# The low halves of a trunk kernel's weight pieces: a negated rounding by ScalarE and an adding transfer instead of subtractions by VectorE and GpSimd

## The chip, the core and the metric

The kernel runs on one core of a Trainium2 chip. The metric is the time of one execution on the device in microseconds (us). The kernel before takes 1647.43 us, the median of 3 runs (1647.31 to 1648.04).

## What is computed

A two-layer encoder trunk is applied to two sequences of 256 tokens with 1024 features each. All weights are fp32 and come from HBM in every run. Per layer, in the reference's words:

```
h = rmsnorm(x, attn_norm[l]);  proj = h @ w_in[l]
a_cols, b_cols, c_cols, d_cols, g_cols = jnp.split(proj, [p1, p2, p3, p4], axis=-1)
o_a, o_b, o_c, o_d = diff_mixer(a_cols ...), natten_mixer(b_cols ...), mla_mixer(c_cols ...), gqa_mixer(d_cols ...)
merged = sum over i of sigmoid(g_cols)[i] * (o_i @ w_branch[l, i])
x = x + merged @ w_out[l]
x = x + conv_ffn(rmsnorm(x, ffn_norm[l]), w_ffn_in[l], ffn_conv_w[l], ffn_conv_b[l], w_ffn_out[l])
```

## The kernel before

All 512 tokens are columns of tiles of 128 partitions x 512. Every weight matrix is cut on the host into **pieces** of 128 partitions x up to 1280 columns, laid one behind the other in one HBM tensor (`wflat`), in the order in which TensorE uses them. There are 131 pieces per layer, 262 in all; most have 1024 columns (512 KB), the gate pieces with a branch block have 1280 (640 KB).

To multiply in fp32 quality with the faster fp32r matmul, every operand is split into a rounded high half and the low rest: `wh` is the weight rounded to fp32r, `wl` is weight minus `wh`. A product is three matmuls, `wh*xh`, `wh*xl`, `wl*xh` (`mm3`, lines 296 to 299; `v_unit`, lines 455 to 457, has the weights as moving operand). So the first use of a piece's `wl` is the third matmul (in `v_unit` the second) on that piece.

One piece is one **unit** of a long list. Per layer in this order: `bq0 bk0 bq1 bk1 vb0 vb1 aq0 ak0 aq1 ak1 vd0 vd1 ve0 ve1 vf0 vf1 va0 va1` (the projections of the four attention branches), `g0` to `g31` with `cq ck cv` between (gates, with the branch products packed in), `gx0 gx1`, `wo0` to `wo7`, `fu0 fg0` to `fu21 fg21` (first half of the feed-forward), `fo0_0` to `fo7_2` (second half). A full unit of 1024 columns is 24 matmuls. The `v` pieces come in twos: unit `ve0` issues no matmul at all, and unit `ve1` issues 96 matmuls that use both pieces in turns, so that `ve1`'s data is first needed 12 matmuls after the start and `ve0`'s buffers are held almost to the end. `wo0` and `wo1` also share their matmuls.

The loop over units at lines 1206 to 1234 sets the program order: unit `i`'s matmuls, then the side work of attention, then `split_piece(i + 2)` and `load_piece(i + 5)`. `load_piece` issues the transfer of a piece from HBM into a `raw` buffer on SyncE's queue. `split_piece` (lines 279 to 294) makes `wh` by an ACTIVATE on ScalarE (line 289) and `wl` by subtraction, first half on VectorE (line 292), second half on GpSimd (line 293). `raw`, `wh` and `wl` have 3 buffers each. So piece `j` writes its `wl` into the buffer that piece `j - 3` leaves, and it can't begin before the last matmul on that piece has run. The tile framework orders the instructions of each engine by a schedule of its own; TensorE's order stays close to the program's. Each engine runs its instructions in that order.

Of the kernel before, what the change touches and what calls it, by code (L numbers as in the profile page):

```python
# [13 lines left out]
AF = mybir.ActivationFunctionType  # L14
ALU = mybir.AluOpType
# [136 lines left out]
def _piece_cols(nm):  # L152
    if nm[0] == "v":
        return {"e": 1152, "f": 1280}.get(nm[1], 1024)
    if nm == "cq":
        return 768
    if nm in ("ck", "cv"):
        return 256
    if nm[:2] == "gx":
        return 256 * (GX[int(nm[2:])][1] - GX[int(nm[2:])][0])  # L160
    if nm[0] == "g":
        return 1280 if int(nm[1:]) in GBR else 1024
    if nm[:2] == "fo":
        return 1024 if nm.endswith("_0") else 896
    return 1024
# [37 lines left out]
def trunk_kernel(ctx: ExitStack, tc: tile.TileContext, xt, wflat, gains, lams, rpb, consts, yt):  # L203
# [14 lines left out]
    V, S, G, PE = nc.vector, nc.scalar, nc.gpsimd, nc.tensor  # L218
# [11 lines left out]
    def f(ap):  # L230
        return ap.bitcast(F32)
# [30 lines left out]
    offs, o = [], 0  # L262
# [3 lines left out]
    raws, splits = {}, {}  # L266
# [12 lines left out]
    def split_piece(i, parts=1, pool_only=False):  # L279
        if i >= len(order):  # L280
            return
        n = _piece_cols(order[i][1])
        raw = raws.pop(i)
        wh = wpool.tile([128, 1280], F32R, tag="wh", name=f"wh{i}", bufs=W_BUFS)
        wl = wpool.tile([128, 1280], F32R, tag="wl", name=f"wl{i}", bufs=W_BUFS)
        w = n // parts
        for q in range(parts):
            a, b = q * w, q * w + w
            S.activation(out=wh[:, a:b], in_=raw[:, a:b], func=AF.Copy)  # L289
            c = a if pool_only else (a + b) // 2  # L290
            if c > a:
                V.tensor_tensor(out=wl[:, a:c], in0=raw[:, a:c], in1=f(wh[:, a:c]), op=ALU.subtract)  # L292
            G.tensor_tensor(out=wl[:, c:b], in0=raw[:, c:b], in1=f(wh[:, c:b]), op=ALU.subtract)  # L293
        splits[i] = (wh, wl)
# [869 lines left out]
    nc.sync.dma_start(out=lv, in_=lams.rearrange("(u n) -> u n", u=1).to_broadcast([128, DEPTH * L_ROW]))  # L1164
    prep(0, gcol(0, G_ATTN), False)
    split_piece(0, 2, True)
    load_piece(RAW_BUFS)
    for d in range(1, ND):
        prep(d, gcol(0, G_ATTN + d), False, d % 2 == 1)
        if d == 2:  # L1170
            split_piece(1, 2)
            load_piece(1 + RAW_BUFS)
# [9 lines left out]
    for i in range(2, LOOK):  # L1182
        split_piece(i)
        load_piece(i + RAW_BUFS)
# [21 lines left out]
    for i, u in enumerate(units):  # L1206
# [7 lines left out]
        wh, wl = splits.pop(i)  # L1214
# [78 lines left out]
```

## Time and profile before

| | |
|---|---|
| median of 3 runs | 1647.43 us |
| the profiled execution's own time | 1647.62 us |
| its span, first to last instruction | 1645.8 us |
| mean granted TensorE clock | 0.989 |
| TensorE (PE) busy | 1615.6 us, 98% |
| VectorE (DVE) busy | 1003.9 us, 61% |
| GpSimd (POOL) busy | 663.1 us, 40% |
| ScalarE (ACT) busy | 634.9 us, 39% |
| read from HBM | 145.77 MB |

The 1.8 us between the span and the execution's time lie around the span. PE's busy time counts pipelined matmuls whose ends are modelled: in the long stages one 512-column matmul starts every 0.227 us though each is shown with 0.39 us. What holds PE up is therefore read from its waits and from the starts of its matmuls.

### The profile page before, as it was taken

How to read it: one execution, taken by the hardware profiler on the slowest of the kernel's cores; microseconds unless marked ns; L12 is line 12 of the kernel's file. 1: busy time of each engine (PE TensorE's matmuls, PEld its weight loads, DVE VectorE, ACT ScalarE, POOL GpSimd, SP SyncE). 2: the span in 40 equal slices, each digit the busy share in tenths (PEclk: the TensorE clock that was granted, in tenths of full speed). 3: DMA queues.
4: the chain of work that ended last, by engine and by line, in shares of the span. 5: the costliest groups of instructions: out<-in, count | busy, mean ns of one | idle time of the engine just before them, and what ended most of it. 6: DMA issues, size and time to landing. Idle time of an engine off the chain costs nothing.

```text
span 1645.8 us, 21201 instructions
## 1 busy us (share of the span) xinstructions
PE 1615.6 (98%) x8035; PEld 1343.8 (82%) x8035; DVE 1003.9 (61%) x1668; ACT 634.9 (39%) x1115; POOL 663.1 (40%) x449
## 2 busy tenths in 40 slices
PE   8989999999999999999998999999999999999997
PEld 6889877878888888888886987888788888888886
DVE  7787585655776666633358675756468666656113
ACT  4555553342323333322234554544333333333321
POOL 4352223444634444444444312234465344444342
PEclk9999999999999999999998999999999999999999
DMA  6222122222323322323331121322222233232331
GB/s 218 84 68 82 55 96 80 80 78 70 107 90 103 98 95 91 98 93 106 101 109 67 55 94 57 108 84 80 77 72 98 90 103 103 90 98 88 106 95 63
DMA packets 50534, 149.24 MB, mean 91 GB/s; under 512 B 13184, under 2 KB 16128, under 8 KB 50432
## 3 DMA queue, kind: packets, MB, share of 16 engines
q1 hardware_dynamic: 49344, 146.84, 27.4%
q8 instruction: 63, 1.03, 0.3%
q10 hardware_dynamic: 1088, 1.05, 0.2%
q14 instruction: 39, 0.32, 0.1%
HBM read 145.77 MB, written 2.10 MB: 90 GB/s over the span
## 4 chain that ended last, share of the span: by engine, by line
PE 93%; DVE 3%; issue 2%; ACT 1%; POOL 0%; DMA 0%; SPq 0%; POOLq 0%; ACTq 0%; DVEq 0%
PE pf L298 10%; PE pf L299 10%; PE pf L297 10%; PE pg L297 7%; PE pg L298 7%; PE pg L299 7%; PE pfo L297 5%; PE pfo L298 5%; PE pfo L299 5%; PE pb L299 2%; PE pwo L299 2%; PE pb L298 2%; PE pwo L298 2%; PE pb L297 2%; PE pwo L297 2%
## 5 line engine op out<-in xcount | busy, mean ns | idle before, releaser
L293 POOL TENSOR_TENSOR wl<-raw,wh 128x512 fp32r<-128x512 f32 (+4 forms) x264 | 449.9, 1705 | 561.7 <-ACT wh L289 439.9
L289 ACT ACTIVATE wh<-raw 128x1024 fp32r<-128x1024 f32 (+5 forms) x264 | 281.7, 1068 | 436.4 <-PE pfo L298 132.3
L292 DVE TENSOR_TENSOR wl<-raw,wh 128x512 fp32r<-128x512 f32 (+4 forms) x262 | 254.1, 970 | 213.6 <-ACT wh L289 203.6
L297 PE MATMUL pf<-xh,wh 128*128 128x512 f32 x704 | 274.3, 390 | 0.0
L299 PE MATMUL pf<-xh,wl 128*128 128x512 f32 x704 | 273.9, 389 | 0.0
L298 PE MATMUL pf<-xl,wh 128*128 128x512 f32 x704 | 273.9, 389 | 0.0
L297 PE MATMUL pg<-xh,wh 128*128 128x512 f32 x512 | 202.2, 395 | 0.1
L298 PE MATMUL pg<-xl,wh 128*128 128x512 f32 x512 | 199.8, 390 | 0.0
L299 PE MATMUL pg<-xh,wl 128*128 128x512 f32 x512 | 199.5, 390 | 0.0
L297 PEld LDWEIGHTS pf<-xh,wh 128*128 128x128 f32 x704 | 132.2, 188 | 27.5
L298 PEld LDWEIGHTS pf<-xl,wh 128*128 128x128 f32 x704 | 132.2, 188 | 27.4
L299 PEld LDWEIGHTS pf<-xh,wl 128*128 128x128 f32 x704 | 132.2, 188 | 27.2
L297 PE MATMUL pfo<-ah,wh 128*128 128x512 f32 (+1 forms) x374 | 141.1, 377 | 0.0
L298 PE MATMUL pfo<-al,wh 128*128 128x512 f32 (+1 forms) x374 | 140.8, 376 | 0.0
L299 PE MATMUL pfo<-ah,wl 128*128 128x512 f32 (+1 forms) x374 | 140.8, 376 | 0.0
L931 POOL TENSOR_TENSOR mg<-mg,gz 128x512 f32<-128x512 f32 x48 | 64.5, 1347 | 165.4 <-DVE gz L930 165.4
L303 POOL TENSOR_TENSOR al<-fc,ah 128x512 fp32r<-128x512 f32 x44 | 57.8, 1314 | 178.9 <-ACT ah L302 178.9
L297 PEld LDWEIGHTS pg<-xh,wh 128*128 128x128 f32 x512 | 96.2, 188 | 21.1 <-issue 0.9
L299 PEld LDWEIGHTS pg<-xh,wl 128*128 128x128 f32 x512 | 96.1, 188 | 20.5
L298 PEld LDWEIGHTS pg<-xl,wh 128*128 128x128 f32 x512 | 96.3, 188 | 18.3
L952 ACT ACTIVATE gz<-gz 128x512 f32<-128x512 f32 x64 | 40.4, 631 | 127.3 <-DVE gz L951 127.2
L788 ACT ACTIVATE pr<-sc,mx 128x256 f32<-128x256 f32 x128 | 59.1, 471 | 78.6 <-DVE mx L783 78.6
(390 smaller groups left out, 2917.5 us busy)
## 6 DMA issues: line engine op xcount, KB each, us to landing
raw<-in_w_dram SPq DMA_DIRECT2D x158, 512.0 KB, 3.3
raw<-in_w_dram SPq DMA_DIRECT2D x58, 640.0 KB, 3.8
raw<-in_w_dram SPq DMA_DIRECT2D x32, 448.0 KB, 3.3
raw<-in_w_dram SPq DMA_DIRECT2D x4, 576.0 KB, 3.4
bias<-in_rpb_dram SPq DMA_DIRECT2D x32, 64.0 KB, 3.5
xall<-in_xt_dram SPq DMA_DIRECT2D x3, 512.0 KB, 7.1
raw<-in_w_dram SPq DMA_DIRECT2D x4, 256.0 KB, 4.5
out_dram<-y SPq DMA_DIRECT2D x4, 256.0 KB, 2.5
```

The lines of the kernel that those rows point to most:

```text
L289: S.activation(out=wh[:, a:b], in_=raw[:, a:b], func=AF.Copy)
L292: V.tensor_tensor(out=wl[:, a:c], in0=raw[:, a:c], in1=f(wh[:, a:c]), op=ALU.subtract)
L293: G.tensor_tensor(out=wl[:, c:b], in0=raw[:, c:b], in1=f(wh[:, c:b]), op=ALU.subtract)
L297: PE.matmul(ps, lhsT=wh, rhs=xh, start=first, stop=False)
L298: PE.matmul(ps, lhsT=wh, rhs=xl, start=False, stop=False)
L299: PE.matmul(ps, lhsT=wl, rhs=xh, start=False, stop=last)
L303: (eng or V).tensor_tensor(out=l, in0=v, in1=f(h), op=ALU.subtract)
L788: S.activation(out=p[:, qt * 256:qt * 256 + 256], in_=src[c][:, qt * 256:qt * 256 + 256], func=AF.Exp, scale=sc, bias=mx[:, i:i + 1], accu ...
L931: G.tensor_tensor(out=m, in0=m, in1=z, op=ALU.add)
L952: S.activation(out=z, in_=z, func=AF.Tanh, scale=0.5)
```

## The change

`split_piece` gets a second way, taken by every piece but the first two (which are split in two parts). ScalarE writes the rounded piece with its sign turned into `wl`, ScalarE writes the rounded piece into `wh`, and a transfer issued by GpSimd reads the piece once more from HBM and adds it onto `wl`. That makes `wl` weight minus rounded weight, as before. The two subtractions are no longer issued for these 260 pieces. Loads, buffers and matmuls are the same.

```
         w = n // parts
+        if not pool_only and parts == 1:
+            src = wflat[offs[i]:offs[i] + 128 * n].rearrange("(p n) -> p n", p=128)
+            S.activation(out=wl[:, :n], in_=raw[:, :n], func=AF.Copy, scale=-1.0)
+            S.activation(out=wh[:, :n], in_=raw[:, :n], func=AF.Copy)
+            G.dma_start(out=wl[:, :n], in_=src, accum_op=ALU.add)
+            splits[i] = (wh, wl)
+            return
         for q in range(parts):
```

Lines behind it stand 7 lower in the changed kernel. There, L289 is the negated rounding, L290 the rounding, L291 the adding transfer.

ScalarE in the first layer where TensorE goes from unit `vd1` to `ve1`, before (`wh_1121` is piece `ve1`, `wh_1149` is `vf0`; `hsq`, `vD` and `ob0h` are attention work, `ptr` a transposed tile):

```order
L814 ACTIVATE ptr<-pt 128x512
L500 ACTIVATE hsq<-psvd 128x128
L505 ACTIVATE vD<-psvd,rs 128x128
L289 ACTIVATE wh_1121<-raw_776 128x1152
L500 ACTIVATE hsq<-psvd 128x128
L505 ACTIVATE vD<-psvd,rs 128x128
L302 ACTIVATE ob0h<-po 128x256
L289 ACTIVATE wh_1149<-raw_872 128x1280
```

The same place of the changed kernel (`wl_1122` is `ve1`'s low half, `wl_1150` is `vf0`'s):

```order
L821 ACTIVATE ptr<-pt 128x512
L507 ACTIVATE hsq<-psvd 128x128
L512 ACTIVATE vD<-psvd,rs 128x128
L289 ACTIVATE wl_1122<-raw_776 128x1152
L507 ACTIVATE hsq<-psvd 128x128
L512 ACTIVATE vD<-psvd,rs 128x128
L290 ACTIVATE wh_1121<-raw_776 128x1152
L507 ACTIVATE hsq<-psvd 128x128
L309 ACTIVATE ob0h<-po 128x256
L289 ACTIVATE wl_1150<-raw_872 128x1280
```

Here the negated rounding stands where the rounding stood, and the rounding two instructions later. On GpSimd at the same place, before (`dr` and `rsh` are rotary work of attention):

```order
L594 TENSOR_TENSOR rsh<-rsh,sinr 128x512
L496 TENSOR_TENSOR dr_896<-dr_896,rtm 128x128
L293 TENSOR_TENSOR wl_1122<-raw_776,wh_1121 128x576
L496 TENSOR_TENSOR dr_897<-dr_897,rtm 128x128
L293 TENSOR_TENSOR wl_1150<-raw_872,wh_1149 128x640
```

And changed:

```order
L503 TENSOR_TENSOR dr_896<-dr_896,rtm 128x128
L291 DMA wl_1122<-in_w_dram 128x1152
L503 TENSOR_TENSOR dr_897<-dr_897,rtm 128x128
L503 TENSOR_TENSOR dr_898<-dr_898,rtm 128x128
L291 DMA wl_1150<-in_w_dram 128x1280
```

The transfer's issue takes the subtraction's place in GpSimd's order. On ScalarE in the feed-forward stage of the first layer, before (`wh_5430` is piece `fg13`, `wh_5475` is `fu14`; `fc`, `fg` and `ah` belong to the feed-forward's evacuation):

```order
L1022 ACTIVATE fg<-fc 128x512
L302 ACTIVATE ah_5392<-fc 128x512
L289 ACTIVATE wh_5430<-raw_5322 128x1024
L289 ACTIVATE wh_5475<-raw_5356 128x1024
L1016 ACTIVATE fc<-fg,gn 128x512
```

And changed:

```order
L1029 ACTIVATE fg<-fc 128x512
L290 ACTIVATE wh_5430<-raw_5322 128x1024
L309 ACTIVATE ah_5392<-fc 128x512
L289 ACTIVATE wl_5431<-raw_5322 128x1024
L290 ACTIVATE wh_5475<-raw_5356 128x1024
L289 ACTIVATE wl_5476<-raw_5356 128x1024
L1023 ACTIVATE fc<-fg,gn 128x512
```

The schedule puts the rounding ahead of the negated rounding here, against the order of the source lines; it does so for 214 of the 260 pieces, in the attention and gate stages not for all, in the stages from `wo` on for nearly all. On ScalarE where `wo0` (`wh_4037`) and `wo1` (`wh_4060`) are split, before:

```order
L952 ACTIVATE gz<-gz 128x512
L289 ACTIVATE wh_4037<-raw_3887 128x1024
L934 ACTIVATE mh_4033<-mg_2730 128x512
L952 ACTIVATE gz<-gz 128x512
L289 ACTIVATE wh_4060<-raw_3931 128x1024
```

And changed:

```order
L959 ACTIVATE gz<-gz 128x512
L290 ACTIVATE wh_4037<-raw_3887 128x1024
L289 ACTIVATE wl_4038<-raw_3887 128x1024
L941 ACTIVATE mh_4033<-mg_2730 128x512
L959 ACTIVATE gz<-gz 128x512
L290 ACTIVATE wh_4060<-raw_3931 128x1024
L289 ACTIVATE wl_4061<-raw_3931 128x1024
```

The negated rounding stands behind the rounding in both. TensorE's order differs in a handful of places of the attention stage by a few rows.

## Rows read from the trace of the kernel before

**Rows 1.** The page's first part: engine, busy us, share of span, instructions.
```profile
PE 1615.6 (98%) x8035; PEld 1343.8 (82%) x8035; DVE 1003.9 (61%) x1668; ACT 634.9 (39%) x1115; POOL 663.1 (40%) x449
```

**Rows 2.** PE's waits: us in total, times, longest us; the longest row.
```profile
PE sc L765 <- DVE sb L776: 9.3, 4, 3.1
```

**Rows 3.** Costliest groups: busy us, mean ns of one, idle before, releaser.
```profile
L293 POOL TENSOR_TENSOR wl<-raw,wh 128x512 fp32r<-128x512 f32 (+4 forms) x264 | 449.9, 1705 | 561.7 <-ACT wh L289 439.9
L289 ACT ACTIVATE wh<-raw 128x1024 fp32r<-128x1024 f32 (+5 forms) x264 | 281.7, 1068 | 436.4 <-PE pfo L298 132.3
L292 DVE TENSOR_TENSOR wl<-raw,wh 128x512 fp32r<-128x512 f32 (+4 forms) x262 | 254.1, 970 | 213.6 <-ACT wh L289 203.6
```

**Rows 4.** DMA queue (packets, MB, share of 16 engines) and issues (median us to landing).
```profile
q1 hardware_dynamic: 49344, 146.84, 27.4%
...
raw<-in_w_dram SPq DMA_DIRECT2D x158, 512.0 KB, 3.3
raw<-in_w_dram SPq DMA_DIRECT2D x58, 640.0 KB, 3.8
```

**Rows 5.** Timeline (start us, us) in the feed-forward, around piece `fg13` (first layer).
```profile
597.78 0.39 PE L299 MATMUL pf<-xh,wl 128*128 128x512 f32 x1
...
599.60 1.04 ACT L289 ACTIVATE wh<-raw 128x1024 fp32r<-128x1024 f32 x1
599.77 1.30 POOL L303 TENSOR_TENSOR al<-fc,ah 128x512 fp32r<-128x512 f32 x1 [4.25 <-ACT ah L302]
...
609.34 0.39 PE L299 MATMUL pf<-xh,wl 128*128 128x512 f32 x1
```

**Rows 6.** Timeline at `ve1`, `vf1`, `va1` (first layer): release, rounding, first use of `wl`.
```profile
98.18 0.28 PE L456 MATMUL psvd<-wl,xh 128*128 128x256 f32 x1
...
98.92 1.16 ACT L289 ACTIVATE wh<-raw 128x1152 fp32r<-128x1152 f32 x1
...
103.19 0.29 PE L456 MATMUL psve<-wl,xh 128*128 128x288 f32 x1
...
113.30 1.27 ACT L289 ACTIVATE wh<-raw 128x1280 fp32r<-128x1280 f32 x1 [1.16 <-PE psve L457]
...
119.13 0.31 PE L456 MATMUL psvf<-wl,xh 128*128 128x320 f32 x1
...
130.93 1.06 ACT L289 ACTIVATE wh<-raw 128x1024 fp32r<-128x1024 f32 x1 [1.08 <-PE psvf L457]
...
135.92 0.28 PE L456 MATMUL psva<-wl,xh 128*128 128x256 f32 x1
```

**Rows 7.** Timeline at `wo0` and `wo1` (first layer): roundings, first uses of `wl`.
```profile
411.64 1.04 ACT L289 ACTIVATE wh<-raw 128x1024 fp32r<-128x1024 f32 x1
...
416.47 1.99 ACT L289 ACTIVATE wh<-raw 128x1024 fp32r<-128x1024 f32 x2
...
417.52 0.39 PE L299 MATMUL pwo<-mh,wl 128*128 128x512 f32 x1
...
420.92 0.39 PE L299 MATMUL pwo<-mh,wl 128*128 128x512 f32 x1
```

**Rows 8.** Timeline at the last piece, `fo7_2`: rounding, first use of `wl`.
```profile
1617.02 0.95 ACT L289 ACTIVATE wh<-raw 128x896 fp32r<-128x896 f32 x1 [3.81 <-PE pfo L298]
...
1622.63 0.28 PE L299 MATMUL pfo<-ah,wl 128*128 128x256 f32 x1
```

**Rows 9.** Attention timeline of PE and DVE; then one stretch by engine, clock, DMA.
```profile
71.33 0.68 DVE L292 TENSOR_TENSOR wl<-raw,wh 128x512 fp32r<-128x512 f32 x1
...
76.86 0.38 PE L765 MATMUL sc<-bk1h,bq1h 64*128 64x256 f32 x1 [1.58 <-DVE sb L776]
...
80.05 1.89 DVE L595 TENSOR_TENSOR rc<-rc,rsh 128x512 f32<-128x512 f32 x1 [1.34 <-POOL rsh L594]
...
90.81 0.58 PE L765 MATMUL sc<-bk1h,bq1h 64*128 64x256 f32 x1 [3.05 <-DVE sb L776]
...
78.24:81.66 3.42, 3.42 (x19) 3.42 (x18) 2.08 (x3) 1.09 (x4) 2.92 (x3) 0.50 0.01 2
```

## The prediction

> **What bounds the kernel now.** I read the busy times first: TensorE is busy for 98% of the span, no other engine for more than 61% [rows 1]. The changed kernel has the same matmuls, so freeing VectorE and GpSimd buys time only where TensorE waits for them. The list of TensorE's waits says how much: its longest row is 9.3 us in four waits, for VectorE in the attention stages [rows 2]. The second thing to read is therefore not who is relieved but how early `wl` is ready, because `wl` stands in front of every third matmul. Three buffers let piece `j` begin its `wl` only when piece `j - 3` is done with, so all the work on `wl` must fit between that release and the first matmul that reads it. I read this budget from timelines of the feed-forward, of the attention projections, of `wo` and of the last piece [rows 5 to 8].
>
> **What is taken away.** 264 subtractions on GpSimd (449.9 us) and 262 on VectorE (254.1 us), but for those of the first two pieces [rows 3]. Nearly all of it is off the path. On the path it counts at two places per layer: VectorE reaches `sb` late and TensorE waits 1.58 and 3.05 us for it [rows 9]. Ahead of the first wait VectorE did two subtractions of 0.68 us [rows 9], so 1.4 us of that go. Ahead of the second stand one subtraction, about 0.7 us, and a rotary add that took 1.89 us, three times the length of an ordinary 512-column VectorE operation of 0.68 us, while GpSimd subtracted beside it [rows 9]; without both the wait loses about 2.0 us. After the first wait the granted clock fell to 0.50, that is 1.2 GHz, for 3.42 us in which TensorE was busy throughout [rows 9]; at 2.4 GHz half of that, 1.7 us, would have done. If the wait is short enough the fall goes too. Together 1.4 + 2.0 + 1.7 = 5.1 us a layer, 10 us in all. The bounds are 0 (ScalarE's longer queue puts the same time back) and 16 us (both waits, 4.6 us, vanish with 3.4 us of slow clock a layer).
>
> **What is added on ScalarE.** 260 activations of about 1.07 us [rows 3], 278 us on an engine that is 39% busy: no bound. But each lies in `wl`'s own chain, and where the rounding is placed ahead of it (214 pieces) there are two activations in the chain, not one. The rounded halves' own readiness moves by one activation at most and is needed later than the sum below; I count nothing for it.
>
> **What is added on GpSimd and the queues.** 260 issues in place of the subtractions. No DMA is issued from GpSimd in this trace, so its cost has to be bounded: 0 from below, and from above the 1.7 us of the subtraction it replaces [rows 3]. I take 1.0 us. What is queued behind an issue on GpSimd, `mg`, `al` and `dr` work, waited behind the subtraction before, so nothing is counted there. The waiting for ScalarE moves with it.
>
> **The adding transfer.** It is the new last link of the chain, and no row shows one. Nearest is the plain load of a piece: 3.3 us from issue to landing for 512 KB, 3.8 us for 640 KB [rows 4]. The queue's row gives the part that scales: 27.4% of 1645.8 us is 451 us for 146.84 MB, 3.07 us per MB, 1.6 us for 512 KB (0.524 MB) and 2.0 us for 640 KB. An add needs the old value, so bytes from two places for every byte written. From below it costs as much as a plain load. I take one load's landing plus the time of a second transfer: 3.3 + 1.6 = 4.9 us (640 KB: 5.8; 576 KB, between the two: 5.2; 448 KB: 4.7). It also meets traffic: ScalarE's last read of `raw` frees that buffer, and the load of the piece three further on (1.6 us) then starts on the same 16 engines. I take half, 0.8 us. The delay from the end of the negated rounding to landed data, call it D, is 1.0 + 4.9 + 0.8 = 6.7 us for 512 KB (640 KB 7.6; 576 KB 7.0; 448 KB 6.5). Its bounds are 3.3 us (no issue time, a plain load, no meeting) and 1.7 + 4.9 + 1.6 = 8.2 us, more if the add itself is slow.
> The Trainium skill, "Collectives: The Full Stack", section on why ReduceScatter is half of AllGather, measured an adding transfer at 1/1.93 of a copy's rate, for two reads on one ring. By that the second transfer would cost 0.93 x 1.6 = 1.5 us in place of 1.6, and the sum would hardly change; no run here shows it.
>
> **Where D fits.** Feed-forward, piece `fg13`: TensorE leaves the buffer at 597.78 + 0.39 = 598.2, and `wl` is first read at 609.34 [rows 5]. In the changed order ScalarE does the rounding, then `ah`, which was over when GpSimd took it at 599.77, then the negated rounding: 599.8 + 1.05 = 600.8. GpSimd is in `al` until 599.77 + 1.29 = 601.1 [rows 5]. Budget 609.3 - 601.1 = 8.2 us against 6.7: it fits, by 1.5 us. `fu` pieces have no `ah` ahead and about 1 us more. The 16 DMA engines bear it too: per unit of 24 x 0.227 = 5.44 us one load and one adding transfer, 1.6 + 3.2 = 4.8 us, 88%. So the long stages, four fifths of the span, should keep their pace.
>
> **Where D doesn't fit.** The `v` pairs hold two of three buffers until their end and then need the next pair's second piece 12 matmuls later [rows 6]. The rounding there now starts at the release, so I put the negated rounding in its place (the changed order has it first there):
> - `ve1`: over at 98.92 + 1.16 = 100.1, read at 103.19; budget 3.1, D 7.0: TensorE waits 3.9 us.
> - `vf1`: 113.30 + 1.27 = 114.6, read at 119.13; 4.5 against 7.6: 3.1 us.
> - `va1`: 130.93 + 1.06 = 132.0, read at 135.92; 3.9 against 6.7: 2.8 us.
> - `wo0`: second on ScalarE, so 411.64 + 1.04 + 1.05 = 413.7, read at 417.52; 3.8 against 6.7: 2.9 us [rows 7].
> - `wo1`: 416.47 + 1.0 + 1.06 = 418.5, read at 420.92, which `wo0`'s wait moves to 423.8; 5.3 against 6.7: 1.4 us [rows 7].
> - Other places with short units (`vb1`, `wo3`, `fo7_1`'s like): an estimate of 2 us a layer.
> That is 16.1 us a layer, 32 for two. The last piece has 1617.02 + 2 x 0.95 = 1618.9 to 1622.63, 3.7 against 6.5: 2.8 us at the very end [rows 8]. Sum 35 us. Each of the three `v` waits is longer than the 1.58 us after which the clock fell; at 1.7 us each that is 5 us a layer, 10 in all, from 0 to twice that.
>
> **The sum.** 35 us of waits, + 10 for the clock, - 10 for the relief: +35 us on the profiled execution's own 1647.62, which is the median of the runs (1647.43) within 0.2 us: 1683 us, 2.1% slower. With D between 6.2 and 7.7 and the two tens moving by 6 against each other it is 1660 to 1705.
>
> **Rivals.**
> First, a **quick transfer**: it lands like a plain load, 3.3 to 3.8 us. With 1.0 us for the issue D is 4.3 to 4.8. Then `ve1` waits 1.3, `vf1` 0.3, `va1` 0.4, `wo0` 0.5, together 2.5 us a layer, and the end 0.6: 5.6 us, with no fall of the clock after waits that short, against 10 us of relief: 1643 us, faster. With relief of only 5 us it is 1648, the same. For it speaks that a 128 KB longer load costs only 0.5 us more [rows 4]; against it, that the old `wl` has to be fetched before it can be added to. It decides from D below about 4.8 us.
> Second, a **long D**: 8.5 to 9 us, by the upper bounds together. The named places grow by 2 us, ten of them and the end make 22 us more, and the feed-forward's budget of 8.2 us breaks by 0.3 to 0.8 us at each of 44 `fg` pieces, 13 to 35 us: 1718 to 1740 us. What can lengthen it here is VectorE: the trace shows VectorE and GpSimd stretching each other (0.68 us becomes 1.89) [rows 9]. The Trainium skill, "SBUF — State Buffer", section "SBUF: two separate sides", says that a DMA issued from GpSimd waits for descriptors while VectorE runs an operation that takes the shared port pair; this rule speaks against the change, and by it each issue could start late by one or two VectorE operations. Priced by rows, one or two operations of 0.68 us at the ten tight places and the end are 7 to 15 us on top of 1683, 1690 to 1698, inside my range; I give it within the chance of this rival and the forecast. No run here shows it yet.
> Third, **the DMA engines become the bound**: from the point where the adding transfer takes 5.44 - 1.6 = 3.8 us of the engines, 2.4 plain transfers. At three (4.8 us) a unit takes 6.4 us for 5.44; some 150 such units (88 `fu` and `fg`, 16 `wo`, 48 `fo`) make +145 us, with the tight places about 1840 us.
> Fourth, **the change doesn't do what it says**: the instructions' order shows the adding transfers on GpSimd and no subtraction for these pieces, so only that the schedule reverses the two activations, which is in the sum.
>
> **Chances.** Forecast (1660 to 1705) 0.55; quick transfer 0.15, of which 0.10 is faster and 0.05 within the bound; long D 0.18; DMA-bound 0.10; none of these 0.02, faster. A measurement of this kernel can tell some 0.2%, 3.3 us, from no change. So faster 0.12, same 0.05, slower 0.83. The range reaches from 1643, the quick transfer's time, to 1760, past the long D: it leaves out the DMA-bound case and the faster half of the quick one.
>
> **What would show it.** Right: adding transfers of 512 KB landing in about 5.7 us after the issue, new waits of TensorE on a DMA of 2.8 to 3.9 us at the `v` pieces and `wo0`, none in the feed-forward, where matmuls still start every 0.227 us; `sb` waits shorter than 9.3 us in total. Wrong: landing under 4 us or above 8; a DMA share near 90% with feed-forward units longer than 5.44 us; new waits on ScalarE's `ptr` or `mh` in place of those on `wl`.

## The result and the profile after

The changed kernel takes 1693.41 us (median; 1689.62 to 1700.76) against 1647.67 us before (median of 4): ratio 1.0283, 95% interval 1.0248 to 1.0318. That is slower by 2.8%, 45.7 us; the prediction was 1683. The profiled execution took 1693.45 us with a span of 1691.7, 45.9 us longer than the span before.

The parts of the page that answer to [rows 1] and [rows 4] (busy times; queues with packets, MB and share of 16 engines; issues with median us to landing):

```profile
PE 1628.2 (96%) x8035; PEld 1351.6 (80%) x8035; DVE 669.0 (40%) x1408; ACT 882.1 (52%) x1375; POOL 428.9 (25%) x449
...
q0 software_dynamic: 37440, 139.48, 46.9%
q1 hardware_dynamic: 49344, 146.84, 28.3%
...
raw<-in_w_dram SPq DMA_DIRECT2D x158, 512.0 KB, 5.3
wl<-in_w_dram POOLq DMA_DIRECT2D x158, 512.0 KB, 7.7
raw<-in_w_dram SPq DMA_DIRECT2D x58, 640.0 KB, 4.8
wl<-in_w_dram POOLq DMA_DIRECT2D x58, 640.0 KB, 8.6
```

VectorE and GpSimd are relieved as promised, by 335 and 234 us, and TensorE's share falls from 98% to 96%. The adding transfer of 512 KB lands 7.7 us after its issue, and the load of `raw`, 3.3 us before, now needs 5.3. TensorE's waits, the view of [rows 2] (us in total, times, longest):

```profile
PE pwo L306 <- DMA wl<-in_w_dram: 13.6, 6, 2.6
PE sc L772 <- DVE sb L783: 7.6, 2, 4.3
PE psva L463 <- DMA wl<-in_w_dram: 7.4, 2, 3.9
PE pt L815 <- ACT ptr L821: 5.8, 2, 2.9
PE psvf L463 <- DMA wl<-in_w_dram: 4.5, 2, 2.4
PE psvb L463 <- DMA wl<-in_w_dram: 3.5, 3, 1.4
PE psve L463 <- DMA wl<-in_w_dram: 3.2, 2, 2.6
PE pfo L306 <- DMA wl<-in_w_dram: 3.0, 3, 2.1
```

The rows on the transfer that writes `wl` are new and come to 35.2 us. One of them, `va1` of the first layer, step by step (start us, us), and then the stretches before, at and after the wait (length, busy us and instructions of PE, PEld, DVE, ACT, POOL, granted clock, DMA share, GB/s):

```profile
135.05 1.06 ACT L289 ACTIVATE wl<-raw 128x1024 fp32r<-128x1024 f32 x1 [0.93 <-PE psvf L463]
...
136.41 0.88 POOL L291 DMA_DIRECT2D wl<-in_w_dram  x1 [15.29 <-ACT wl L289]
...
144.27 0.58 PE L463 MATMUL psva<-wl,xh 128*128 128x256 f32 x1 [3.92 <-DMA wl<-in_w_dram]
```
```profile
134.00:140.00 6.00, 6.00 (x46) 5.28 (x46) 1.13 (x3) 5.07 (x16) 1.75 (x2) 1.00 0.27 48
140.00:144.00 4.00, 0.35 (x3) 0.14 (x2) 2.53 (x8) 2.17 (x6) 0.00 (x0) 0.90 1.03 246
144.00:150.00 6.00, 5.73 (x27) 5.73 (x28) 0.86 (x2) 1.39 (x5) 0.00 (x0) 0.50 0.49 142
150.00:156.00 6.00, 6.00 (x52) 6.00 (x52) 2.90 (x15) 2.15 (x7) 0.00 (x0) 1.00 0.00 0
```

The negated rounding ends at 136.1, GpSimd issues 0.3 us later, and the matmul that reads `wl` starts at 144.27: D, from the end of the negated rounding to the landed data, is 8.2 us. TensorE stood still for 3.92 us, and in the six us behind that it ran 27 matmuls at clock 0.50 where the next six hold 52. So this one wait costs nearly 7 us. In the wait itself the DMA engines are full (share 1.03): beside this transfer the loads of two later pieces (issued at 137.08 and 141.71) and the next piece's adding transfer (138.94) are on their way.

In the feed-forward, piece `fg13` again ([rows 5]), and 130 us of that stage:

```profile
617.65 1.04 ACT L289 ACTIVATE wl<-raw 128x1024 fp32r<-128x1024 f32 x1
...
619.07 0.87 POOL L291 DMA_DIRECT2D wl<-in_w_dram  x1
...
627.41 0.39 PE L306 MATMUL pf<-xh,wl 128*128 128x512 f32 x1
```
```profile
490.00:620.00 130.00, 130.00 (x577) 107.63 (x577) 51.44 (x74) 71.86 (x84) 35.83 (x36) 1.00 0.85 191
```

577 matmuls in 130 us are 0.225 us each, the pace of before, with the DMA engines at 85%. From the issue to the first use there are 8.3 us here, and the transfer fits.

**Where 45.9 us went.** Three sums per kernel come from its trace: the waits on the transfer that writes `wl`, the other waits, and an estimate of what the clock took, as span x (1 - mean granted clock). The mean clock was 0.989 before and is 0.982 now: 18.1 and 30.5 us. Waits on `wl` +35.2, clock +12.4, `sb` -1.7, `ptr` +1.4, other waits -2.4: 44.9 of 45.9. The same sums for every run below, in us:

| kernel | span | waits on wl | sb | ptr | other | clock |
|---|---|---|---|---|---|---|
| before | 1645.8 | 0 | 9.3 | 4.4 | 9.8 | 18.1 |
| after | 1691.7 | 35.2 | 7.6 | 5.8 | 7.4 | 30.5 |
| e1_rest | 1653.1 | 4.7 | 6.3 | 6.6 | 8.1 | 19.8 |
| e2_tight | 1700.8 | 35.2 | 9.3 | 4.4 | 10.0 | 37.4 |
| e3_copy | 1645.4 | 4.9 | 5.8 | 5.7 | 7.9 | 16.5 |
| e5_noraw | 1671.3 | 20.1 | 8.6 | 5.7 | 7.1 | 23.4 |
| e6_rt | 1691.5 | 36.8 | 0 | 5.6 | 14.4 | 25.4 |
| e8_before_rt | 1643.6 | 0 | 5.2 | 7.5 | 10.4 | 13.1 |
| e9_ahead | 1645.2 | 0.2 | 7.7 | 6.2 | 8.2 | 14.8 |
| e10_ahead_rt | 1642.9 | 3.5 | 0 | 5.8 | 10.7 | 14.8 |
| e11_ahead_rt5 | 1645.7 | 2.0 | 0.9 | 6.7 | 9.1 | 19.7 |
| e13_before_rt5 | 1642.9 | 0 | 5.7 | 6.0 | 9.9 | 16.4 |

What is left of each span is 1604 to 1609 us, so these columns hold the large differences. They do not settle differences of a few us between the later runs: the clock is printed to 0.001, which is 1.7 us.

### The profile page after: what moved, and what is told of

It reads as the page before. It is cut to its first block, busy times and chain, and to the rows that moved or that the text cites. A ratio compares the mean times of both kernels' runs of the same rounds, so it can differ in the third digit from the quotient of the medians.

```text
span 1691.7 us, 21217 instructions
## 1 busy us (share of the span) xinstructions
PE 1628.2 (96%) x8035; PEld 1351.6 (80%) x8035; DVE 669.0 (40%) x1408; ACT 882.1 (52%) x1375; POOL 428.9 (25%) x449
## 3 DMA queue, kind: packets, MB, share of 16 engines
q0 software_dynamic: 37440, 139.48, 46.9%
q8 instruction: 63, 1.03, 0.2%
## 4 chain that ended last, share of the span: by engine, by line
PE 79%; DMA 7%; issue 7%; DVE 3%; POOL 2%; ACT 1%; SPq 1%; POOLq 0%; DVEq 0%; ACTq 0%
PE pf L304 9%; PE pf L306 9%; PE pf L305 9%; PE pg L304 7%; PE pg L305 7%; PE pg L306 7%; DMA wl<-in_w_dram 6%; PE pfo L306 3%; PE pfo L304 3%; PE pfo L305 3%; PE pb L306 2%; PE pb L304 2%; PE pb L305 2%; PE pt L815 1%; PE po L869 1%
## 5 line engine op out<-in xcount | busy, mean ns | idle before, releaser
L290 ACT ACTIVATE wh<-raw 128x1024 fp32r<-128x1024 f32 (+4 forms) x260 | 279.9, 1077 | 410.0 <-issue 244.5
L291 POOL DMA_DIRECT2D wl<-in_w_dram x260 | 227.6, 875 | 799.5 <-ACT wl L289 756.7
L289 ACT ACTIVATE wl<-raw 128x1024 fp32r<-128x1024 f32 (+4 forms) x260 | 277.1, 1066 | 9.7 <-PE psve L463 2.2
L1021 DVE TENSOR_TENSOR fg<-pf,rsrow 128x512 f32<-128x512 f32 x44 | 30.4, 691 | 169.2 <-PE pf L306 169.2
```

The lines of the kernel that those rows point to most:

```text
L289: S.activation(out=wl[:, :n], in_=raw[:, :n], func=AF.Copy, scale=-1.0)
L290: S.activation(out=wh[:, :n], in_=raw[:, :n], func=AF.Copy)
L291: G.dma_start(out=wl[:, :n], in_=src, accum_op=ALU.add)
L1021: V.tensor_tensor(out=g, in0=D.pop(("f", j, 1)), in1=st["row"], op=ALU.mult)
```

## The experiments

Theory: the loss sits where the first use of `wl` comes sooner than D, about 8 us, after the negated rounding, and D is long because of the add and because it meets the load of `raw`. Rivals: the traffic or ScalarE's longer queue costs everywhere; starting a transfer from GpSimd is what is long.

### Which places lose: e1_rest and e2_tight

```
# e1_rest
+        tight = order[i][1][0] == "v" or order[i][1][:2] == "wo" or order[i][1][:3] == "fo7"
+        if not pool_only and parts == 1 and not tight:
# e2_tight
+        tight = order[i][1] in ("vb1", "ve1", "vf1", "va1", "wo0", "wo1", "wo3", "fo7_1", "fo7_2")
+        if not pool_only and parts == 1 and tight:
```

> The v pieces, wo0 to wo7 and the three fo7 pieces get the subtraction back (21 of 143 pieces a layer); all others keep the negated rounding and the adding transfer. Theory (the loss is TensorE's wait at first uses of wl that come sooner than the transfer, about 8 us after the negated rounding): nearly all of the 35 us of waits on wl and of the slow clock behind them go, 1645 to 1655 us, the same as before. Rival (the traffic of some 220 adding transfers, the HBM reads and ScalarE's longer queue cost everywhere): a good part stays, 1665 us or more.

Measured 1654.38 us, ratio 1.0040 (1.0025 to 1.0055). (A layer has 131 pieces, not 143.) With 218 of the 260 adding transfers still there, 39 of the 46 us are gone. The 4.7 us of waits on `wl` that remain lie at places I had not listed (an `ak` piece behind a `v` pair, 2.3 us, five `fo` pieces, 2.0, and a gate piece, 0.4). The rival is out as the main cause.

> The reverse: only vb1, ve1, vf1, va1, wo0, wo1, wo3, fo7_1 and fo7_2 (18 pieces of 286) have the adding transfer, the others the subtraction. Theory (a tight place loses by the transfer's own length, whatever the neighbours do): landing stays at 7 us or more for 512 KB and the waits stay within 1 us each of those with all pieces changed, together 25 to 35 us, 1675 to 1692 us. Rival (the length comes from traffic, two transfers on the queue and the raw loads beside them): landing falls below 6 us, the waits lose about 2 us each, 1655 to 1668 us.

Measured 1701.56 us, ratio 1.0327 (1.0312 to 1.0343): 18 adding transfers, of 262 pieces, cost no less than all 260 (1.0283, 1.0248 to 1.0318). The sum of the waits and the landing are as the theory has them, though single waits differ by up to 2.7 us (`ve1` of the second layer, 3.3 against 0.7); the time is above its range. The waits of this kernel:

```profile
PE pwo L307 <- DMA wl<-in_w_dram: 10.4, 4, 3.0
PE sc L773 <- DVE sb L784: 9.3, 4, 3.1
PE psva L464 <- DMA wl<-in_w_dram: 7.8, 2, 4.1
PE psve L464 <- DMA wl<-in_w_dram: 7.3, 2, 4.0
```

Its issues (median us to landing) and its mean clock:

```profile
wl<-in_w_dram POOLq DMA_DIRECT2D x10, 512.0 KB, 7.3
```
```profile
core 0: 1700.8 us, clock 0.978
```

The waits on `wl` are 35.2 us, as with all pieces changed; there 1.8 of the 35.2 stood at pieces outside these 18. With almost no neighbour of its own kind, but beside the loads of `raw`, the transfer still needs 7.3 us. What I missed is the clock: 37.4 us against 18.1 before, more than the 30.5 of the full change. Nine of this kernel's twelve waits on `wl` of over 0.9 us come with a stretch of 3.4 us at clock 0.50, but only five of the full change's fifteen (of 3.4 or 6.8 us). Why the other ten there do not is not shown. VectorE's four waits on `sb`, 9.3 us, are all there in addition.

### What makes the transfer long: e3_copy and e5_noraw

```
# e3_copy
-            G.dma_start(out=wl[:, :n], in_=src, accum_op=ALU.add)
+            G.dma_start(out=wl[:, :n], in_=src)
# e5_noraw (raw: three fixed buffers)
+        raw = rawp[i % 3]
+        if i < 3:
+            nc.sync.dma_start(out=raw[:, 1024:], in_=wflat[:128 * 256].rearrange("(p n) -> p n", p=128))
+        else:
+            n, parts = 64, 1
```

> Same order, but GpSimd's transfer writes wl without adding (wl is then the weight itself, the low half is not computed). Theory as predicted (the add costs the time of a second transfer, 1.6 us, and the meeting): landing of 512 KB 7.7 - 1.6 = 6.1 us, some 20 waits lose 1.6 us each, about 1660 us. Rival one (starting a transfer from GpSimd is what is long): landing 7.2 us or more, 1688 us or more. Rival two (the add is most of it): landing 5 us or less, 1655 us or less.

Measured 1648.63 us, ratio 1.0007 (0.9996 to 1.0018): no slower than before. Queue, GpSimd's instruction and landing:

```profile
q0 software_dynamic: 37440, 139.48, 24.6%
...
L291 POOL DMA_DIRECT2D wl<-in_w_dram x260 | 142.9, 550 | 823.4 <-ACT wl L289 782.7
...
raw<-in_w_dram SPq DMA_DIRECT2D x158, 512.0 KB, 3.3
wl<-in_w_dram POOLq DMA_DIRECT2D x158, 512.0 KB, 4.4
```

The issues from 1605 us on, which are those of the last three pieces and have no load of `raw` beside them, since none is left to issue:

```profile
wl<-in_w_dram POOLq DMA_DIRECT2D x2, 448.0 KB, 3.5
wl<-in_w_dram POOLq DMA_DIRECT2D x1, 512.0 KB, 3.5
```

Rival two holds. From GpSimd a plain copy lands in 4.4 us beside a load, and `raw` is not delayed beside it; with no load beside it, it lands in 3.5 us, 0.2 more than a load from SyncE. The add makes 7.7 of 4.4, and its issue holds GpSimd for 0.88 us in place of 0.55. In engine time the copy takes 0.246 x 1645.4 us for 139.48 MB, 2.90 us per MB; the add 0.469 x 1691.7, 5.69 us per MB: 1.96 times.

> The loads of raw after the third piece fetch 64 columns in place of 1024 (both halves are then rounded from other weights' values); the adding transfers are whole. Theory as predicted (a transfer that meets the raw load loses 0.8 us): landing 6.9 us, some 20 waits lose 0.8 us each, about 1677 us. Rival one (raw loads do not matter): landing 7.5 us or more, 1688 us or more. Rival two (the meeting is the main thing): landing 5.5 us or less, 1660 us or less.

Measured 1671.67 us, ratio 1.0147 (1.0130 to 1.0164). Its issues:

```profile
wl<-in_w_dram POOLq DMA_DIRECT2D x158, 512.0 KB, 5.2
wl<-in_w_dram POOLq DMA_DIRECT2D x58, 640.0 KB, 5.9
```

The add beside loads of 64 columns lands in 5.2 us; the meeting with the whole loads is worth 2.5 us, not 0.8. The landing is that of rival two, the time lies between it and mine: at D = 5.5 us the tight places still wait for 20.1 us.

### More time in place of a shorter transfer: e9_ahead

```
+        wl = wpool.tile([128, 1280], F32R, tag="wl", name=f"wl{i}", bufs=4)
...
         split_piece(i + LOOK)
         load_piece(i + LOOK + RAW_BUFS)
+        low_piece(i + LOOK + 1)
```

`low_piece` holds the negated rounding and the adding transfer; `split_piece` keeps the rounded half.

> The changed kernel with a fourth wl buffer: the negated rounding and the adding transfer are issued three pieces ahead, the rounded half two ahead as before (two of the 60 work tiles pay for the space). Theory (the loss is budget against a transfer delay of 8 us): each tight place gains at least 3 us, the 35 us of waits on wl fall below 8, the slow clock behind them goes, 1643 to 1655 us. Rival (ScalarE, which waits in order for raw and for the wl buffer, hands the delay on to ptr and to the evictions, or the traffic costs anyway): 1662 us or more.

Measured 1649.23 us, ratio 1.0007 (0.9998 to 1.0016). One wait on `wl` is left, and the issues land sooner. In the median the adding transfer is now issued 1.2 us behind the nearest load of `raw`, where it was 0.3 us in the changed kernel; that this is why it lands sooner is not tested:

```profile
PE sc L779 <- DVE sb L790: 7.7, 2, 4.3
PE pt L822 <- ACT ptr L828: 5.9, 2, 2.9
...
PE psbq L313 <- DMA wl<-in_w_dram: 0.2, 1, 0.2
```
```profile
raw<-in_w_dram SPq DMA_DIRECT2D x158, 512.0 KB, 3.5
wl<-in_w_dram POOLq DMA_DIRECT2D x158, 512.0 KB, 5.8
```

The theory holds, and the run shows something else: with all waits on `wl` gone, the change does not gain anything over the kernel before. VectorE is free of 260 subtractions, and the time is the same.

### Where the relief went: e6_rt, e8_before_rt, e10, e11, e13

In the changed kernel's attention stage (first layer), VectorE and GpSimd:

```profile
80.97 0.57 DVE L613 CAST aq1p<-aq1h 32x512 fp32r<-32x512 f32 x1
81.56 5.37 DVE L613 CAST aq1p<-aq1l 32x512 fp32r<-32x512 f32 x1
86.94 0.42 DVE L613 CAST aq1p<-aq1h 32x512 fp32r<-32x512 f32 x1
```
```profile
80.71 0.92 POOL L291 DMA_DIRECT2D wl<-in_w_dram  x1 [2.75 <-ACT wl L289]
81.30 0.56 POOL L481 COPY rt<-cst 128x32 f32<-128x32 f32 x1
...
85.33 1.31 POOL L484 TENSOR_TENSOR rt<-cst,lv 128x256 f32<-128x256 f32 x2
```

A copy that takes 0.42 us takes 5.37 while GpSimd builds the `rt` tables, twelve operations without a gap from 81.30 to 86.64. In the kernel before, the same twelve also run without a gap, from 81.32 to 89.42, but the casts beside them take at most 0.85 us:

```profile
81.32 0.68 POOL L474 COPY rt<-cst 128x32 f32<-128x32 f32 x1
...
86.36 0.85 DVE L606 CAST aq1p<-aq1l 32x512 fp32r<-32x512 f32 x1
...
87.84 1.58 POOL L477 TENSOR_TENSOR rt<-cst,lv 128x256 f32<-128x256 f32 x2
```

Why VectorE and GpSimd take turns there and not here is not shown. To see whether the tables are what holds the cast, the tables were moved from `vd0` to the third piece of the layer, in the changed kernel (e6_rt), in the kernel before (e8_before_rt) and in e9_ahead (e10_ahead_rt); then to `vb1` (e11_ahead_rt5, e13_before_rt5).

```
-        specs["vd0"] = (lambda wh, wl: (pv(wh, wl), tabs()), None)
+        specs["vd0"] = (pv, None)
+        p1, e1 = specs[names[2]]
+        specs[names[2]] = (lambda wh, wl: (p1(wh, wl), tabs()), e1)
```

> The changed kernel with GpSimd's work on the rt tables moved from piece vd0 to the third piece of the layer, tens of us earlier. Theory (the relief of VectorE was lost because a cast that takes 0.42 us took 5.37 us while GpSimd worked on rt back to back behind the transfer's issue): the cast is back under 1 us, the waits on sb fall from 7.6 to 4 us or less, and with the clock behind them 1684 to 1690 us. Rival (ScalarE's negated rounding ahead of the copies is what delays sb): the waits on sb stay at 7 us or more and the time at 1691 to 1696 us.

Measured 1693.66 us, ratio 1.0284 (1.0270 to 1.0298): unchanged. The same cast, two of the waits, and a VectorE operation of the second layer:

```profile
83.92 0.42 DVE L613 CAST aq1p<-aq1l 32x512 fp32r<-32x512 f32 x1
```
```profile
PE psve L463 <- DMA wl<-in_w_dram: 6.4, 2, 4.1
PE sc L772 <- ACT bk0h L309: 6.2, 1, 6.2
```
```profile
862.78 7.88 DVE L310 TENSOR_TENSOR bq0l<-bc,bq0h 128x512 fp32r<-128x512 f32 x1 [6.43 <-ACT bq0h L309]
```

That the tables beside it hold the cast is shown: no cast of this kind takes over 0.6 us any more and no wait on `sb` is left. The gain that I expected is not there. `ve1`, the next tight place, waits 6.4 us in place of 3.2. And another VectorE operation now stands: in the second layer `bq0l` takes 7.88 us, where its like (`bk0l` behind it) takes 0.69, while GpSimd works without a gap on the moved `rt` tables, `cosr`, `sinr` and `bias`; `bk0h` waits behind it, and TensorE waits 6.2 us for `bk0h`.

> The kernel before with the same move of the rt tables. Control: if the tables hold VectorE up there too, sb waits of 9.3 us fall by 1 to 3 us and the time to 1643 to 1646 us; if the subtractions are what holds it, no change, 1646 to 1649 us.

Measured 1644.54 us, ratio 0.9979 (0.9970 to 0.9988): the time is that of the first case; the `sb` waits fall by 4.1 us, more than it has, `ptr` takes 3.1 of them back, and less time is spent at the slow clock.

> The kernel with four wl buffers and the rt tables moved as well. Theory: the two effects add, 3 to 8 us under the run with four buffers alone, 1638 to 1650 us. Rival: with no waits on wl the tables no longer meet the cast, and nothing is gained.

Measured 1644.68 us, ratio 0.9987 (0.9978 to 0.9996), 4.5 us under e9_ahead. With the waits on `wl` nearly gone, the move does pay, but it only comes to the time of e8_before_rt (1644.54), which has the move and not the change.

> Four wl buffers, adding transfers three pieces ahead, and the rt tables at vb1, where VectorE and GpSimd are least busy, in place of the third piece. Theory (the rt work costs by what it collides with): the waits on sb stay gone as with the earlier move, and the new ones at the third piece (3.5 us on wl, 1.9 on bk0l, 2.7 on wh) go too: 1636 to 1643 us. Rival (a wait that goes is handed to the next one on TensorE's way, ptr or a wl): 1643 to 1648 us.

Measured 1646.14 us, ratio 0.9992 (0.9983 to 1.0001). The time is the rival's: `sb` waits 0.9, but `ptr` 6.7, and the clock took 19.7 us. Of the waits that were to go, the one on `bk0l` is gone, 2.0 on `wl` and 2.5 on `wh` are left.

> Control: the kernel before, with the rt tables at vb1. If the gain over the kernel before is the tables' alone, it comes to the same time as the run above within 3 us; if the adding transfers relieve VectorE in addition, the run above is 3 to 8 us faster than this one. Expected here 1642 to 1646 us.

Measured 1644.83 us, ratio 0.9984 (0.9975 to 0.9993). Against e11_ahead_rt5 no gain of the adding transfers is to be seen. Three versions beat the kernel before, by 0.1 to 0.2%: e8_before_rt, e13_before_rt5 and e10_ahead_rt, and the first two do it without the change.

## Why the prediction came out as it did

**The mechanism was right.** The waits on `wl` at the `v` pieces, `wo` and the last piece are there, the first half of the feed-forward keeps its pace, and slow clock stands behind some of the long waits. The sum of the waits was put at 35 us and is 35.2.

**Single terms were not.** D was put at 6.7 us and is 8.0 to 8.2. Its parts by e3_copy and e5_noraw: issue and plain landing, 1.0 + 3.3 = 4.3, measured 3.5; the second read 1.6, measured 1.7 (3.5 to 5.2); the meeting with `raw` 0.8, measured 7.7 - 5.2 = 2.5. The meeting was the mis-sized term. I halved the load's engine time, but the add brings 3.0 us of engine time (5.69 x 0.524 MB) to the load's 1.6, and both fall on the same release. A copy, with half of that engine time, loses only 0.9 us beside a load (3.5 to 4.4).
That the sum of the waits still fits is luck in part: errors that cancel. Budgets were taken from the places of before, each by itself, and a wait ahead of a place gives it time: `ve1` (3.9 predicted, 2.6 and 0.7 us in the two layers) stands behind the `sb` wait of 4.3 and 3.3 us, and e6_rt shows it at 6.4 in total when that wait is gone. `vf1` came in under the estimate too (4.5 us for two against 6.2), and the last piece (2.1 against 2.8). `va1` came in over it (7.4 against 5.6), `wo0` and `wo1` close to it (8.9 against 8.6), and the places that had only a flat 4 us for both layers (`vb0`, `vb1`, `wo3`, two `fo` pieces) took 9.1.

**The clock**: +10 predicted, +12.4 measured, and this too is luck in part. The 10 stood for the six `v` waits. Three of them brought slow clock, 13.6 us at 0.50, which costs half of it, 6.8; `wo3` and the last piece, for which nothing was counted, brought 10.2 us, which cost 5.1.

**The relief is the step that failed**: -10 us (6.8 of waits, 3.4 of clock), measured -2.7 of waits (`sb` -1.7, `ptr` +1.4, others -2.4) and nothing of the clock: around these places it stands at 0.50 for 10.2 us in the first layer and 13.7 in the second, before 10.2 and 13.6. Two of the four `sb` waits went, as predicted for the 1.58 us ones. The two others grew from 3.05 [rows 9] to 4.3 and 3.3. The rotary add did lose its stretch (0.69 in place of 1.89 us), but the `rt` tables held one cast for 5.37 us. VectorE still came to `sb` earlier, at 89.03 in place of 90.08 us; TensorE stood there from 85.5 in place of 87.8. The -2.7 lies near the lower bound, 0, for which I had named ScalarE; the cause shown is another. Of the 10.4 us between 1683 and the profiled 1693.45, 7.3 are this relief and 2.4 the clock.

**Rivals.** The quick transfer is what e3_copy shows: with a landing of 4.4 us the time is that of before, and even then no 10 us are gained. Long D was nearer to the chip than the forecast's 6.7, but the feed-forward's budget did not break at 8.2: `fg13` had 8.3 us from the issue alone. The DMA engines did not become the bound: the adding transfer takes 1.96 plain transfers of engine time, less than the 2.4 of that rival, and they carried 85%, against the 88% estimated.
The Trainium skill, "Collectives: The Full Stack", section on why ReduceScatter is half of AllGather, gives a factor of 1.93 between AllGather, which copies, and ReduceScatter, which adds. The engine time here agrees: 1.96. The 1.5 us that the prediction estimated from it for the second read agrees too where no load is beside the transfer: 1.7 us (3.5 to 5.2).
The Trainium skill, "SBUF — State Buffer", section "SBUF: two separate sides", has the rule that a transfer from GpSimd starves while VectorE holds the shared port. The runs show no sign of it in the landing: in e5_noraw the add of 512 KB lands in 5.1 us where VectorE is busy for 39% (490 to 620 us) and in 5.2 at the end, where it is busy for 9%. The same section says that of certain VectorE operations and a GpSimd operation the one that starts first gets the shared pair of ports for the whole instruction and the other is blocked. The cast of 5.37 us looks like that, but it stood through twelve GpSimd instructions and not one.

## What to carry to other kernels

A transfer with an add is priced by what lands beside it: here it took twice the engine time of a copy, and when the same event released the next load, both arrived late. Before moving work from an engine to a DMA, list the first uses that come within the transfer's delay; a few of them (18 of 262 pieces here) can carry the whole loss, and here one buffer more took it away. Taking load off an engine gained nothing by itself here: waits that went were met by others, and GpSimd's other work held VectorE at a new place.

## What the runs showed of the hardware that I had not expected

- An adding transfer of 512 KB lands in 5.2 us with little else on the DMA engines and in 7.7 beside a load, which then needs 5.3 in place of 3.3. A plain copy from GpSimd needs 3.5 alone and 4.4 beside the same load, and the load keeps its 3.3.
- GpSimd is held for 0.88 us by the issue of an adding transfer and for 0.55 us by that of a copy of the same shape.
- A VectorE copy of 0.42 us was held for 5.37 us through twelve GpSimd operations in a row; in the kernel before the same twelve ran in a row too, and the copies beside them took at most 0.85 us. In e6_rt a VectorE subtraction of 0.69 us was held for 7.88.
- The 35.2 us of waits in e2_tight brought an estimated 19.3 us of slow clock with them, the 35.2 us of the full change 12.4. At `va1` of the changed kernel TensorE had stood still for 3.92 us and was then granted 0.50, that is 1.2 GHz, for the next six us, 5.73 of them busy.
